# PEER gates by indirect writes into a DRAM table of experts, in place of a grid in SBUF

## The chip, the cores and the metric

One core of a Trainium2 chip. The metric is the device time of one execution of the program in microseconds (us); lower is better. Engines: TensorE (PE), VectorE (DVE), ScalarE (ACT), GpSimd (POOL) and SyncE (SP). SP, ACT and POOL issue DMAs.

## The reference

One decoder layer for 256 tokens of width 1024: two attention branches, a gated merge, then a PEER layer. This part is the PEER layer and what follows it:

```python
q = (ht @ w_pq).reshape(T, 8, 2, 128)
sub = einsum('thpc,hpnc->thpn', q, peer_keys)        # 128 keys per half
s_top, i_top = top_k(sub, 16)
cand_s = s_top[:, :, 0, :, None] + s_top[:, :, 1, None, :]   # 16 x 16 per head
cand_i = i_top[:, :, 0, :, None] * 128 + i_top[:, :, 1, None, :]
best_s, pos = top_k(cand_s, 16)
expert = take_along_axis(cand_i, pos)                # 8 heads x 16 = 128 slots per token
gate = softmax(best_s)
act = gelu(ht . peer_u[expert])
out = sum over slots of gate * act * peer_v[expert]
x = rms_norm(x + gt2 * out, g_final)
```

There are 16384 experts, numbered 128 i + j. A token picks 128 slots; two heads may pick the same expert, whose gates then add up.

## The kernel before, in words

The PEER layer is computed densely. The activations gelu(h . u) of all experts and all 256 tokens are made on PE, weighted by a gate that is zero where a token did not pick the expert, and multiplied by all of v. Experts go by blocks of 128 with one j and all i on the partitions: 128 blocks of u and 128 of v, each [128, 1024] float32 (512 KB), taken in 64 pairs. Every product is in three matmuls of high and low halves (`mm3`, L84 to L87), and each loaded block is split into those halves by one ACT copy (L81) and one DVE subtraction (L82).

1. **0 to 301 us**: adaLN, attention, merge, projection to queries.
2. **301 to 467 us, routing**, in two halves of 128 tokens (`tt`): scores (psub, L650), top 16 on DVE (`top16`, L631), ranks to indices (eq, sel). The result, per token and slot the indices i and j and the gate, is transposed (psel, L716) into `selT`. Between the pieces `u_some` (L589) issues pairs of u blocks: 2.5 units of routing work per pair (`PACE_R`).
3. **467 to 694 us, grid**: for 4 tokens at a time DVE builds one-hot matrices E, A (L746) and B (E times the gate in three bf16 pieces, L753); 12 matmuls pg (L737) per pair of tokens' blocks sum them into [i, token, j], and ACT copies that into the SBUF grid `G` (L740, 128 KB per partition). Two such steps stand between pairs of u blocks (`PACE_G` = 2).
4. **694 to 1081 us, v stage**: 64 pairs of v blocks in the order of a list `order`. `act_of` (L778) brings the activations of a pair, `weighted` (L786) multiplies them by the gates of G and splits the product, `v_mm` adds into four PSUM tiles `acc`. Within it 6 pairs of u blocks are still computed and used directly (j of 116 and above, `J0`); the 58 others were stored by ACT.
5. **to 1099 us**: the sum is scaled by gt2, added to x, normalized and stored. The row form of gt2 is made by 8 products `pgt` (L823) with diagonal matrices `dg` from DVE, within the last three pairs.

The lines that the steps touch:

```python
def u_spill(j):                                                              # L582
    a = upool.tile([P, 2, T], F32, tag="a", name=f"as{j}")
    nc.scalar.activation(a, upair(j, f"s{j}"), AF.Gelu_apprx_tanh)
    nc.scalar.dma_start(act_spill[j // 2], a.rearrange("p a t -> p (a t)"))
...
def act_of(j):                                                               # L778
    a = apl.tile([P, 2, T], F32, tag="a", name=f"a{j}")
    if j < J0:
        nc.sync.dma_start(a.rearrange("p a t -> p (a t)"), act_spill[j // 2])
    else:
        nc.scalar.activation(a, upair(j, f"m{j}"), AF.Gelu_apprx_tanh)
    return a
def weighted(j, a):                                                          # L786
    nc.vector.tensor_mul(a, a, G[:, :, j : j + 2].rearrange("p t s -> p s t"))
```

What sets the order: the program's order of instructions is made per engine by a scheduler, which may move an instruction ahead of others where its inputs allow. Each engine and each of the DMA-issuing queues then works strictly in order. SP loads u, v and the stored activations; a loaded block takes one of four buffers (`raw`), which is free again when the DVE subtraction has read it.

Of the kernel before, what the change touches and what calls it, by code (L numbers as in the profile page):

```python
# [18 lines left out]
P = 128  # L19
# [6 lines left out]
J0 = 116  # L26

PACE_R = 2.5
PACE_G = 2.0
# [5 lines left out]
def kernel(  # L35
# [32 lines left out]

    act_spill = dpool.tile([J0 // 2, P, 2 * T], F32, name="act_spill")
    x1_spill = dpool.tile([2, P, D], F32, name="x1_spill")  # L70
# [419 lines left out]
    for p in range(2):  # L490
        o = pm.tile([P, T], F32, tag="mm", name=f"pd{p}")
        for tt in range(2):
            rest = dilated(p, o, tt)
            gates(4 * p + 2 * tt)
            bg()
            rest()
            gates(4 * p + 2 * tt + 1)
            bg()
        put_o(o, 4 + p, f"d{p}")
# [81 lines left out]

    def u_spill(j):  # L582
        a = upool.tile([P, 2, T], F32, tag="a", name=f"as{j}")
        nc.scalar.activation(a, upair(j, f"s{j}"), AF.Gelu_apprx_tanh)
        nc.scalar.dma_start(act_spill[j // 2], a.rearrange("p a t -> p (a t)"))
# [3 lines left out]
    def u_some(share):  # L589
        spilled[1] += share  # L590
        while spilled[1] >= 1.0 and spilled[0] < J0:
            u_spill(spilled[0])
            spilled[0] += 2
            spilled[1] -= 1.0
# [12 lines left out]
    qT = rpool.tile([P, 16, T], F32, name="qT")  # L607
    ranks = rpool.tile([P, 16, P], BF16, name="ranks")
# [34 lines left out]
    for tt in range(2):  # L643
# [3 lines left out]
        for q in range(4):  # L647
# [11 lines left out]
            u_some(4.0 / PACE_R)  # L659
        nc.vector.tensor_copy(i_top, i_u)  # L660
# [53 lines left out]
        ps = pr_.tile([P, 3, P], F32, tag="t", name=f"psel{tt}")  # L714
        for x in range(3):
            nc.tensor.transpose(ps[:, x], sel[:, x].rearrange("p h k -> p (h k)"), ident)  # L716
        ts_ = slice(P * tt, P * tt + P)
        nc.scalar.activation(selT[:, 0:3, ts_], ps, AF.Copy)
        rest = rpool.tile([P, P], F32, tag="rk", bufs=2, name=f"rest{tt}")
        nc.vector.tensor_sub(rest, ps[:, 2], selT[:, 2, ts_])  # L720
        nc.vector.tensor_copy(selT[:, 3, ts_], rest)
        nc.vector.tensor_sub(selT[:, 4, ts_], rest, selT[:, 3, ts_])
    es_r.close()
    es_x.close()


    gpool = ctx.enter_context(tc.tile_pool(name="grid", bufs=1))
    G = gpool.tile([P, T, NJ], F32, name="G")
    es_g = ExitStack()
    opool = es_g.enter_context(tc.tile_pool(name="onehot", bufs=2))  # L730
    pg = es_g.enter_context(tc.tile_pool(name="pg", bufs=3, space=PSUM))
    def grid_mm(b, A, Bs):

        ps = pg.tile([P, 4, P], F32, tag="g", name=f"pg{b}")
        for t in range(4):
            for x in range(3):
                nc.tensor.matmul(  # L737
                    ps[:, t], A[:, :, t], Bs[t // 2][:, x, :, t % 2], start=(x == 0), stop=(x == 2)
                )
        nc.scalar.activation(G[:, 4 * b : 4 * b + 4], ps, AF.Copy)  # L740

    for b in range(T // 4):
        E = opool.tile([P, P, 4], BF16, tag="E", bufs=1, name=f"E{b}")
        A = opool.tile([P, P, 4], BF16, tag="A", bufs=2, name=f"A{b}")
        for x, M in ((1, E), (0, A)):
            nc.vector.tensor_tensor(  # L746
                M, selT[:, x, None, 4 * b : 4 * b + 4].to_broadcast([P, P, 4]), iota4, op=OP.is_equal
            )
        Bs = []
        for q in range(2):  # L750
            B = opool.tile([P, 3, P, 2], BF16, tag="B", bufs=4, name=f"B{b}_{q}")
            g = selT[:, 2:5, None, 4 * b + 2 * q : 4 * b + 2 * q + 2].to_broadcast([P, 3, P, 2])
            nc.vector.tensor_tensor(  # L753
                B, E[:, None, :, 2 * q : 2 * q + 2].to_broadcast([P, 3, P, 2]), g, op=OP.mult
            )
            Bs.append(B)
        grid_mm(b, A, Bs)
        u_some(1.0 / PACE_G)
    u_some(J0)
    es_g.close()  # L760
# [8 lines left out]
    direct, stored = list(range(J0, NJ, 2)), list(range(0, J0, 2))  # L769
    order = [direct.pop(0)]  # L770
    while direct or stored:
        if direct:
            order.append(direct.pop(0))
        for _ in range(-(-len(stored) // (len(direct) + 1))):
            order.append(stored.pop(0))
    n_pairs = len(order)

    def act_of(j):  # L778
        a = apl.tile([P, 2, T], F32, tag="a", name=f"a{j}")
        if j < J0:  # L780
            nc.sync.dma_start(a.rearrange("p a t -> p (a t)"), act_spill[j // 2])
        else:
            nc.scalar.activation(a, upair(j, f"m{j}"), AF.Gelu_apprx_tanh)
        return a

    def weighted(j, a):  # L786
        nc.vector.tensor_mul(a, a, G[:, :, j : j + 2].rearrange("p t s -> p s t"))  # L787
        wh = wpool.tile([P, 2, T], F32R, tag="wh", name=f"wh{j}")
        wl = wpool.tile([P, 2, T], F32R, tag="wl", name=f"wl{j}")
        split(wh, wl, a)  # L790
        return wh, wl
# [9 lines left out]
    for n, j in enumerate(order):  # L801
# [6 lines left out]
        if n == n_pairs - 3:  # L808
# [3 lines left out]
            ones = wpool.tile([P, P], F32, name="ones")  # L812
            nc.vector.memset(ones, 1.0)
            nc.sync.dma_start(gfb, g_final.to_broadcast([P, D]))
            nc.scalar.activation(gfb, gfb, AF.Copy, scale=float(D**0.5))
            nc.sync.dma_start(x1, x1_spill.rearrange("a p d -> p a d"))
            for q in range(2):
                ps = pp.tile([P, 4, P], F32, tag="pp", name=f"pgt{q}")
                for k in range(4):
                    dg = wpool.tile([P, P], F32, tag="dg", name=f"dg{q}{k}")  # L820
                    i = 40 + 4 * q + k
                    nc.vector.tensor_scalar(dg, ident, mod[:, i : i + 1], None, op0=OP.mult)
                    nc.tensor.matmul(ps[:, k], ones, dg, start=True, stop=True)  # L823
                nc.vector.tensor_copy(gtb[:, 512 * q : 512 * q + 512], ps.rearrange("p a b -> p (a b)"))
# [12 lines left out]
    st = wpool.tile([P, 2, 8], F32, tag="dg", name="st")  # L837
# [37 lines left out]
def _arrays(inputs):  # L875
# [48 lines left out]
    a["iota"] = np.tile(np.repeat(i, 4)[None, :], (P, 1)).astype(ml_dtypes.bfloat16)  # L924
# [29 lines left out]
```

## Time and profile before

| | |
|---|---|
| median of three runs | 1100.81 us (1100.40 to 1103.03) |
| the profiled execution | 1100.67 us, with a span of 1098.9 us |
| PE busy | 1063.5 us, 97% |
| DVE busy | 832.3 us, 76% |
| ACT busy | 557.4 us, 51% |
| POOL busy | 0.2 us |
| moved by DMA | 237.58 MB, mean 216 GB/s |

Busy shares are means over the stages above; what bounds a stage is read from that stage. Matmuls are pipelined, so the sum of their durations is more than the time they take; the distance between their starts is their pace.

### The profile page before, as it was taken

How to read it: one execution, taken by the hardware profiler on the slowest of the kernel's cores; microseconds unless marked ns; L12 is line 12 of the kernel's file. 1: busy time of each engine (PE TensorE's matmuls, PEld its weight loads, DVE VectorE, ACT ScalarE, POOL GpSimd, SP SyncE). 2: the span in 40 equal slices, each digit the busy share in tenths (PEclk: the TensorE clock that was granted, in tenths of full speed). 3: DMA queues.
4: the chain of work that ended last, by engine and by line, in shares of the span. 5: the costliest groups of instructions: out<-in, count | busy, mean ns of one | idle time of the engine just before them, and what ended most of it. 6: DMA issues, size and time to landing. Idle time of an engine off the chain costs nothing.

```text
span 1098.9 us, 19552 instructions
## 1 busy us (share of the span) xinstructions
PE 1063.5 (97%) x7672; PEld 973.4 (89%) x7674; DVE 832.3 (76%) x1539; ACT 557.4 (51%) x706; POOL 0.2 (0%) x4
## 2 busy tenths in 40 slices
PE   7889999998999999999999999999999999999986
PEld 4878988998999999999999999888888888878865
DVE  6777886776799799778777787676777677677675
ACT  5496344655465545545454454544444444445432
POOL 0000000000000000000000000000000000000000
PEclk9999999999999999999999999999999999999998
DMA  9965567365866766755555555567676666668751
GB/s 334 370 222 177 185 230 266 105 211 210 297 220 221 244 206 198 246 181 189 175 191 175 183 183 182 190 216 253 212 249 225 235 220 239 221 222 276 255 195 39
DMA packets 74206, 237.58 MB, mean 216 GB/s; under 512 B 8449, under 2 KB 8833, under 8 KB 73986
## 3 DMA queue, kind: packets, MB, share of 16 engines
q1 hardware_dynamic: 64898, 220.04, 59.1%
q10 hardware_dynamic: 9216, 16.29, 4.0%
q8 instruction: 60, 0.98, 0.4%
q14 instruction: 32, 0.26, 0.1%
HBM read 219.00 MB, written 17.30 MB: 215 GB/s over the span
## 4 chain that ended last, share of the span: by engine, by line
PE 69%; DMA 8%; DVE 5%; issue 3%; ACT 1%; DVEq 0%; SPq 0%; ACTq 0%
PE pus L85 10%; PE pus L86 10%; PE pus L87 10%; PE acc L87 7%; PE acc L86 7%; PE acc L85 7%; DMA a<-act_spill 6%; PE pg L737 4%; DVE l_v L82 1%; DVE wl L82 1%; DMA r_pq<-in_w_pq_dram 1%; PE p_g L85 1%; PE p_g L86 1%; PE pum L87 1%; PE pum L85 1%
## 5 line engine op out<-in xcount | busy, mean ns | idle before, releaser
L85 PE MATMUL pus<-hh_n,h_u 128*128 128x256 f32 x928 | 265.7, 286 | 0.0
L86 PE MATMUL pus<-hl_n,h_u 128*128 128x256 f32 x928 | 262.6, 283 | 0.0
L87 PE MATMUL pus<-hh_n,l_u 128*128 128x256 f32 x928 | 262.4, 283 | 0.0
L81 ACT ACTIVATE h_u<-r_u 128x1024 fp32r<-128x1024 f32 x128 | 135.8, 1061 | 179.4 <-PE pus L86 151.1
L87 PE MATMUL acc<-h_v,wl 128*128 128x512 f32 x512 | 200.9, 393 | 1.0 <-DVE wl L82 0.6
L86 PE MATMUL acc<-l_v,wh 128*128 128x512 f32 x512 | 200.8, 392 | 0.6 <-DVE l_v L82 0.6
L85 PE MATMUL acc<-h_v,wh 128*128 128x512 f32 x512 | 200.1, 391 | 0.0
L81 ACT ACTIVATE h_v<-r_v 128x1024 fp32r<-128x1024 f32 x128 | 134.9, 1055 | 113.7 <-PE acc L87 56.5
L86 PEld LDWEIGHTS pus<-hl_n,h_u 128*128 128x128 f32 x928 | 178.0, 192 | 0.0
L87 PEld LDWEIGHTS pus<-hh_n,l_u 128*128 128x128 f32 x928 | 177.9, 192 | 0.0
L82 DVE TENSOR_TENSOR l_u<-r_u,h_u 128x1024 fp32r<-128x1024 f32 x128 | 155.1, 1219 | 30.1 <-ACT h_u L81 29.9
L85 PEld LDWEIGHTS pus<-hh_n,h_u 128*128 128x128 f32 x928 | 177.8, 192 | 0.0
L82 DVE TENSOR_TENSOR l_v<-r_v,h_v 128x1024 fp32r<-128x1024 f32 x128 | 154.2, 1220 | 15.2 <-ACT h_v L81 15.2
L787 DVE TENSOR_TENSOR a<-a,G 128x512 f32<-128x512 f32 x64 | 70.3, 1099 | 98.1 <-DMA a<-act_spill 98.1
L87 PEld LDWEIGHTS acc<-h_v,wl 128*128 128x128 f32 x512 | 96.5, 189 | 23.7 <-DVE wl L82 4.1
L86 PEld LDWEIGHTS acc<-l_v,wh 128*128 128x128 f32 x512 | 96.7, 189 | 21.6 <-DVE l_v L82 1.9
L85 PEld LDWEIGHTS acc<-h_v,wh 128*128 128x128 f32 x512 | 96.6, 189 | 19.7
L753 DVE TENSOR_TENSOR B<-E,selT 128x768 bf16<-128x768 bf16 x128 | 68.1, 552 | 33.1 <-PE pg L737 33.1
L81 ACT ACTIVATE wh<-a 128x512 fp32r<-128x512 f32 x64 | 40.4, 631 | 81.1 <-PE acc L86 74.8
L151 DVE SCALAR_TENSOR_TENSOR junk<-ada,c_sb 128x1024 bf16<-128x1024 f32 x44 | 53.6, 1218 | 2.8 <-DMA ada<-in_w_ada_dram 2.7
L737 PE MATMUL pg<-B,A 128*128 128x128 bf16 x768 | 52.0, 222 | 1.0 <-DVE rest L720 1.0
L737 PEld LDWEIGHTS <-A 128*128 128x128 bf16 x768 | 46.9, 114 | 2.5 <-issue 1.0
(319 smaller groups left out, 1809.4 us busy)
## 6 DMA issues: line engine op xcount, KB each, us to landing
r_u<-in_u_dram SPq DMA_DIRECT2D x128, 512.0 KB, 3.6
r_v<-in_v_dram SPq DMA_DIRECT2D x128, 512.0 KB, 4.4
ada<-in_w_ada_dram SPq DMA_DIRECT2D x20, 1024.0 KB, 7.4
act_spill<-as ACTq DMA_DIRECT2D x58, 256.0 KB, 2.3
a<-act_spill SPq DMA_DIRECT2D x58, 256.0 KB, 3.7
r_g<-in_w_in_dram SPq DMA_DIRECT2D x16, 512.0 KB, 4.0
r_pq<-in_w_pq_dram SPq DMA_DIRECT2D x16, 512.0 KB, 6.3
r_first<-in_w_in_dram SPq DMA_DIRECT2D x8, 512.0 KB, 7.1
```

Of the source, the lines that this page charges most:

```text
L81: nc.scalar.activation(hi, src, AF.Copy)
L82: last_split[:] = [nc.vector.tensor_sub(lo, src, hi.bitcast(F32))]
L85: nc.tensor.matmul(ps, lh, rh, start=start, stop=False)
L86: nc.tensor.matmul(ps, lh, rl, start=False, stop=False)
L87: nc.tensor.matmul(ps, ll, rh, start=False, stop=stop)
L151: nc.vector.scalar_tensor_tensor(junk, raw[:, k], 1.0, c_sb, op0=OP.mult, op1=OP.mult, accum_out=mod[:, t + k : t + k + 1])
L737: nc.tensor.matmul(ps[:, t], A[:, :, t], Bs[t // 2][:, x, :, t % 2], start=(x == 0), stop=(x == 2))
L753: nc.vector.tensor_tensor(B, E[:, None, :, 2 * q : 2 * q + 2].to_broadcast([P, 3, P, 2]), g, op=OP.mult)
L787: nc.vector.tensor_mul(a, a, G[:, :, j : j + 2].rearrange("p t s -> p s t"))
```

## The change

The gates no longer make a grid. A DRAM table `ag` has a row of 512 float32 for every expert (2 KB), with four parts of 128: for each half of the tokens the activations (x = 0) and the gates (x = 1).

- 32 DMAs on POOL write zeros over all gate parts, 1024 pieces of 512 B each; 16 are issued in the attention, 16 with the first eight pairs of u blocks.
- ACT stores the activations of all 64 pairs into the table, two DMAs per pair, in pieces of 512 B. No pair is left for the v stage.
- Per half of the tokens DVE forms the expert's number of each slot, finds the first slot with the same number (`max_index`), and for each of the 128 slots sums the gates of the slots with the same number. Then POOL writes that slot's 128 sums, one per token, each to its own address of the table: 128 indirect DMAs of 128 single float32. A slot that repeats an earlier one writes to a spare place behind the table. `PACE_G` = 15 of these stand between pairs of u blocks.
- A load `a` brings activations and gates of a pair together (512 KB, 4 KB per partition; four buffers in place of two). It waits for all 256 indirect writes and its pair's own stores.
- The rows of gt2 are made in the routing (`gate_rows`), stored, and loaded at the end. The grid, its one-hot matrices and psel are gone.

```diff
-PACE_G = 2.0
+PACE_G = 15.0
...
+    ag = dpool.tile([NE + SPARE, ROW], F32, name="ag")
...
+    def clear(after):
+        j = blank.pop(0)
+        with tc.issue_after(after.ins):
+            for h in range(2):
+                o = nc.gpsimd.dma_start(
+                    ag_parts[:, j : j + 8, h, 1], zero[:, None, :].to_broadcast([P, 8, P])
+                )
...
     def u_spill(j):
-        nc.scalar.dma_start(act_spill[j // 2], a.rearrange("p a t -> p (a t)"))
+        for s in range(2):
+            o = nc.scalar.dma_start(ag_parts[:, j + s, :, 0], a[:, s].rearrange("p (h t) -> p h t", h=2))
...
+        if blank:
+            clear(made)
...
+    def gate_rows():
+        go = rpool.tile([P, D], F32, tag="xo", bufs=1, name="go")
+        for q in range(2):
+            ps = pr_.tile([P, 4, P], F32, tag="t", name=f"pgt{q}")
+            for k in range(4):
...
+                nc.vector.tensor_scalar(dg, ident, mod[:, i : i + 1], -1.0, op0=OP.mult, op1=OP.mult)
+                nc.tensor.matmul(ps[:, k], neg_one, dg, start=True, stop=True)
+            nc.scalar.activation(go[:, 512 * q : 512 * q + 512], ps.rearrange("p a b -> p (a b)"), AF.Copy)
+        nc.scalar.dma_start(x1_spill[2], go)
...
+        for k in range(0, P, 8):
+            nc.vector.max_index(seen[:, k : k + 8], num[:, k : k + 8], num)
...
+        for k in range(P):
+            same = rpool.tile([P, P], F32, tag="same", name=f"same{tt}_{k}")
+            nc.vector.scalar_tensor_tensor(
+                same, num, num[:, k : k + 1], gf, op0=OP.is_equal, op1=OP.mult, accum_out=tot[:, k : k + 1]
+            )
+            o = nc.gpsimd.indirect_dma_start(
+                out=ag_flat, out_offset=bass.IndirectOffsetOnAxis(ap=at_i[:, k : k + 1], axis=0),
+                in_=tot[:, k : k + 1], in_offset=None,
+            )
...
+            scatters.append(o.ins)
+            u_some(1.0 / PACE_G)
...
-        grid_mm(b, A, Bs)
-        u_some(1.0 / PACE_G)
-    u_some(J0)
+    u_some(NJ)
...
     def act_of(j):
-        a = apl.tile([P, 2, T], F32, tag="a", name=f"a{j}")
-        if j < J0:
-            nc.sync.dma_start(a.rearrange("p a t -> p (a t)"), act_spill[j // 2])
-        else:
-            nc.scalar.activation(a, upair(j, f"m{j}"), AF.Gelu_apprx_tanh)
+        a = apl.tile([P, 2, 2, 2, P], F32, tag="a", bufs=4, name=f"a{j}")
+        o = nc.sync.dma_start(a.rearrange("p s h x t -> p s (h x t)"), ag_pairs[:, j : j + 2])
+        for i in scatters + spills[j]:
+            tc.add_manual_dep(o.ins, i.name, data_dep)
         return a
```

The order of instructions changes in three places that the prediction speaks of.

POOL, the whole program, as it now is (`idle` is a tile of zeros, `tot` the sums, `at_i` the addresses; L212 is the clear, L788 the indirect write):

```order
L969 ISA
L969 MEMSET const-float32-0.0 128x1
L969 MEMSET const-float32-1.0 128x1
L969 MEMSET const-bfloat16-1.0 128x1
L969 MEMSET const-uint8-127 128x1
L975 UNCONDITIONAL_BRANCH
L212 DMA ag<-idle 128x8x128 x32
L788 DMA ag<-tot_4490,at_i_4488 8421376x1 x128
L788 DMA ag<-tot_6601,at_i_6599 8421376x1 x128
L975 UNCONDITIONAL_BRANCH
L975 ISA
```

Before, POOL had the first six and the last of these and no DMA. Each DMA from the ninth on also waits for the eighth before it to land.

SP around the first load of activations, before:

```order
L91 DMA r_u118_8990<-in_u_dram 128x1024
L91 DMA r_u119_9020<-in_u_dram 128x1024
L91 DMA r_v116_9063<-in_v_dram 128x1024
L91 DMA r_v117_9069<-in_v_dram 128x1024
L91 DMA r_v118_9106<-in_v_dram 128x1024
L91 DMA r_v119_9112<-in_v_dram 128x1024
L91 DMA r_v0_9149<-in_v_dram 128x1024
L91 DMA r_v1_9155<-in_v_dram 128x1024
L91 DMA r_v2_9192<-in_v_dram 128x1024
L781 DMA a0_9061<-act_spill_69 128x512
```

and now (r_u96 is block 96 of u; a0, a2 the activations and gates of the first pairs):

```order
L97 DMA r_u96_7771<-in_u_dram 128x1024
L97 DMA r_u97_7801<-in_u_dram 128x1024
L97 DMA r_u98_7836<-in_u_dram 128x1024
L97 DMA r_u99_7866<-in_u_dram 128x1024
L813 DMA a0_8824<-ag_69 128x1024
L97 DMA r_u100_7901<-in_u_dram 128x1024
L813 DMA a2_8826<-ag_69 128x1024
L97 DMA r_u101_7931<-in_u_dram 128x1024
L813 DMA a4_8840<-ag_69 128x1024
L97 DMA r_u102_7966<-in_u_dram 128x1024
L813 DMA a6_8884<-ag_69 128x1024
L97 DMA r_u103_7996<-in_u_dram 128x1024
```

The first load of activations stood behind all loads of u but those of the direct pairs; it now stands ahead of r_u100 to r_u127, and eight such loads are spread among these.

DVE while the second half's slots are summed (L785 the sums, l_u the low half of a u block), where the grid's E, A and B stood between the l_u:

```order
L785 SCALAR_TENSOR_TENSOR same1_50_6947,tot1_6601<-num1_6574,sel1_6267 128x128
L88 TENSOR_TENSOR l_u79_7003<-r_u79_7000,h_u79_7002 128x1024
L785 SCALAR_TENSOR_TENSOR same1_51_6950,tot1_6601<-num1_6574,sel1_6267 128x128
L785 SCALAR_TENSOR_TENSOR same1_52_6953,tot1_6601<-num1_6574,sel1_6267 128x128
L785 SCALAR_TENSOR_TENSOR same1_53_6956,tot1_6601<-num1_6574,sel1_6267 128x128
L785 SCALAR_TENSOR_TENSOR same1_54_6959,tot1_6601<-num1_6574,sel1_6267 128x128
L785 SCALAR_TENSOR_TENSOR same1_55_6962,tot1_6601<-num1_6574,sel1_6267 128x128
L88 TENSOR_TENSOR l_u80_7083<-r_u80_7080,h_u80_7082 128x1024
```

Five sums stand between two subtractions, from block 70 to block 95; the first half's stand so from block 26 to block 48.

## Rows read from the trace of the kernel before

**Rows 1.** The page: busy time by engine; the span in 40 slices.

```profile
PE 1063.5 (97%) x7672; PEld 973.4 (89%) x7674; DVE 832.3 (76%) x1539; ACT 557.4 (51%) x706; POOL 0.2 (0%) x4
...
PE   7889999998999999999999999999999999999986
...
GB/s 334 370 222 177 185 230 266 105 211 210 297 220 221 244 206 198 246 181 189 175 191 175 183 183 182 190 216 253 212 249 225 235 220 239 221 222 276 255 195 39
```

**Rows 2.** Busy time by stage: from:to, length, then each engine; clock, DMA share.

```profile
301.00:467.00 166.00, 165.83 (x1388) 165.73 (x1387) 147.25 (x513) 93.42 (x106) 0.00 (x0) 1.00 0.67 222
467.00:694.00 227.00, 226.20 (x2252) 224.77 (x2252) 178.98 (x312) 113.52 (x159) 0.00 (x0) 1.00 0.55 183
694.00:1081.00 387.00, 380.61 (x1792) 317.35 (x1790) 267.51 (x275) 182.01 (x207) 0.00 (x0) 0.99 0.67 224
```

**Rows 3.** The chain that ended last, in order of time: start, length, what.

```profile
467.80 0.88 PE pg L737 x12
...
472.19 1.46 PE pg L737 x24
...
479.45 1.47 PE pg L737 x24
...
690.07 2.36 PE pg L737 x36
```

**Rows 4.** Groups by line, whole span: count, busy us, mean ns, idle before.

```profile
L753 DVE TENSOR_TENSOR B<-E,selT 128x768 bf16<-128x768 bf16 x128 | 68.1, 552 | 33.1 <-PE pg L737 33.1
...
L740 ACT ACTIVATE G<-pg 128x512 f32<-128x512 f32 x64 | 35.4, 594 | 1.5 <-PE pg L737 1.3 <-ACT G L740 0.2
...
L746 DVE TENSOR_TENSOR E<-selT,iota 128x512 bf16<-128x512 bf16 x64 | 27.0, 421 | 1.1
```

**Rows 5.** Groups by line: DVE in the routing, and ACT's split of u.

```profile
L82 DVE TENSOR_TENSOR l_u<-r_u,h_u 128x1024 fp32r<-128x1024 f32 x57 | 68.4, 1217 | 17.2 <-ACT h_u L81 16.9
...
L641 DVE FIND_INDEX8 i_u<-s_top,sub 128x8 uint32<-128x128 f32 x32 | 8.5, 284 | 0.0
...
L694 DVE SCALAR_TENSOR_TENSOR rk<-pn,pw 128x128 f32<-128x128 uint32 x4 | 1.1, 283 | 0.0
...
L81 ACT ACTIVATE h_u<-r_u 128x1024 fp32r<-128x1024 f32 x128 | 135.8, 1061 | 179.4 <-PE pus L86 151.1
```

**Rows 6.** PE in order of time near the end, and a table as rows 2.

```profile
1062.37 0.39 PE L85 MATMUL acc<-h_v,wh 128*128 128x512 f32 x1
1062.60 0.39 PE L86 MATMUL acc<-l_v,wh 128*128 128x512 f32 x1
...
1068.77 0.80 PE L823 MATMUL pgt<-dg,ones 128*128 128x128 f32 x2 [4.87 <-DVE dg L822]
...
1068.80:1074.30 5.50, 5.50 (x16) 4.63 (x17) 3.22 (x7) 0.00 (x0) 0.00 (x0) 0.50 0.01 2
```

**Rows 7.** Waits, longest in total: who for whom, us, times, longest.

```profile
DVE a L787 <- DMA a<-act_spill: 98.1, 57, 3.6
```

**Rows 8.** Instructions of pus and psel with first and last start; psub's group.

```profile
L85 PE MATMUL pus<-hh_n,h_u x928: 279/283/365, 301.9 to 689.6; 128*128 128x256 f32 x186
...
L716 PE MATMUL psel<-ident,sel x6: 272/272/273, 379.6 to 464.3; 128*128 128x128 f32 x6
...
L650 PE MATMUL psub<-kT,qT 128*128 128x128 f32 x64 | 8.4, 275 | 0.0
```

**Rows 9.** DMA queues, issues to landing, and the issuing queues' own time (ns).

```profile
q10 hardware_dynamic: 9216, 16.29, 4.0%
...
r_u<-in_u_dram SPq DMA_DIRECT2D x128, 512.0 KB, 3.6
...
act_spill<-as ACTq DMA_DIRECT2D x58, 256.0 KB, 2.3
...
L585 ACTq DMA_DIRECT2D act_spill<-as x58: 326/326/334, 310.9 to 691.6; - x58
...
940.18 1.46 SPq L91 DMA_DIRECT2D r_v<-in_v_dram  x2
```

More of the change, by code (lines that the diff above doesn't have):

```diff
@@ L196, in bg @@
                     background.pop(0)()
+    zero = idle.bitcast(F32)[:, 0:P]
+    blank = list(range(0, NJ, 8))
+    def clear(after):
[5 more added lines that the diff above has]
+                )
+                tc.declare_no_dep(o.ins, group="clear", reason="other places")
+                tc.add_to_no_dep_group("clear", o.ins)
     def rms(sq, name):
@@ L580, in upair @@
         return ps
+    spills, scatters = {}, []
     def u_spill(j):
[L583 to L585 removed]
+        a = upool.tile([P, 2, T], F32, tag="a", bufs=2, name=f"as{j}")
+        made = nc.scalar.activation(a, upair(j, f"s{j}"), AF.Gelu_apprx_tanh)
+        spills[j] = []
+        for s in range(2):
+            o = nc.scalar.dma_start(ag_parts[:, j + s, :, 0], a[:, s].rearrange("p (h t) -> p h t", h=2))
+            for g in ("clear", "acts", "gates"):
+                tc.declare_no_dep(o.ins, group=g, reason="other places")
+            tc.add_to_no_dep_group("acts", o.ins)
+            spills[j].append(o.ins)
+        if blank:
+            clear(made)
     spilled = [0, 0.0]
@@ L590, in u_some @@
         spilled[1] += share
-        while spilled[1] >= 1.0 and spilled[0] < J0:
+        while spilled[1] >= 1.0 and spilled[0] < NJ:
             u_spill(spilled[0])
@@ L713 @@
         nc.vector.tensor_tensor(ge, ge, gsum[:, :, None].to_broadcast([P, 8, 16]), op=OP.mult)
[L714 to L720, printed above, removed]
@@ new lines @@
+        nc.vector.tensor_sub(at_f, at_f, spare)
+        nc.vector.tensor_mul(at_f, at_f, fst)
+        at_i = sel_pool.tile([P, P], I32, tag="at_i", bufs=2, name=f"at_i{tt}")
+        nc.vector.tensor_add(at_i, at_f, spare)
+        tot = sel_pool.tile([P, P], F32, tag="tot", bufs=2, name=f"tot{tt}")
+        gf = ge.rearrange("p h k -> p (h k)")
+        for k in range(P):
+            same = rpool.tile([P, P], F32, tag="same", name=f"same{tt}_{k}")
+            nc.vector.scalar_tensor_tensor(
+                same, num, num[:, k : k + 1], gf, op0=OP.is_equal, op1=OP.mult, accum_out=tot[:, k : k + 1]
+            )
+            o = nc.gpsimd.indirect_dma_start(
+                out=ag_flat, out_offset=bass.IndirectOffsetOnAxis(ap=at_i[:, k : k + 1], axis=0),
+                in_=tot[:, k : k + 1], in_offset=None,
+            )
+            for g in ("acts", "gates"):
+                tc.declare_no_dep(o.ins, group=g, reason="other places")
+            tc.add_to_no_dep_group("gates", o.ins)
+            scatters.append(o.ins)
+            u_some(1.0 / PACE_G)
@@ L723 @@
     es_r.close()
     es_x.close()
[L727 to L740, printed above, removed]
@@ L811 @@
             x1 = hpool.tile([P, 2, D], F32, tag="hl", name="x1")
-            ones = wpool.tile([P, P], F32, name="ones")
-            nc.vector.memset(ones, 1.0)
             nc.sync.dma_start(gfb, g_final.to_broadcast([P, D]))
             nc.scalar.activation(gfb, gfb, AF.Copy, scale=float(D**0.5))
[L816 to L824, printed above, removed]
+            nc.sync.dma_start(gtb, x1_spill[2])
+            nc.sync.dma_start(x1, x1_spill[0:2].rearrange("a p d -> p a d"))
         todo = [(w, vs)] if n < n_pairs - 1 else todo + [(w, vs)]
@@ L923, in _arrays @@
     a["cst"] = np.concatenate([np.eye(P), -tri, np.tile(i[None, 0:16], (P, 1))], axis=1).astype(np.float32)
-    a["iota"] = np.tile(np.repeat(i, 4)[None, :], (P, 1)).astype(ml_dtypes.bfloat16)
+    at = [P + 2 * P * h + i for h in range(2)] + [NE * ROW + P * (P * h + i) for h in range(2)]
+    a["iota"] = np.concatenate([np.tile(i[None, :], (P, 1)), np.stack(at, axis=1)], axis=1).astype(np.float32)
     inv = np.float32(10000.0) ** (-np.arange(32, dtype=np.float32) / np.float32(32))
```

66 lines of the change are left out of this document (32 added, 34 removed).

## The prediction

> **What bounds the kernel now.** I read the page's first two parts, then a table by stage, then the chain in order of time, and last the operations that the change replaces. TensorE (PE) is busy 97% of the span and at 9 tenths in nearly every slice [rows 1]. By stage it is the same everywhere the change works, at the full granted clock (1.00, 2.4 GHz) [rows 2]: 165.83 of 166 us while the routing runs, 226.20 of 227 us while the gate grid is built, 380.61 of 387 us while v is multiplied. So an operation on PE between 301 and 1081 us costs its own time, and work on VectorE (DVE) or ScalarE (ACT) costs nothing until it holds PE up. DVE is the nearest: 147 of 166 us in the routing. The DMA engines are 0.55 to 0.67 busy there.
>
> The chain from 467 us on shows it in detail [rows 3]: 24 matmuls of the grid (pg) every 7.26 us for 1.46 us, and between them one pair of u blocks. So a pair of u blocks takes 7.26 - 1.46 = 5.8 us of PE, one block 2.9 us. Two blocks are 1 MB of u.
>
> **The grid's removal.** 768 matmuls pg leave PE. The first and last of their pieces in the chain are 0.88 us (12) and 2.36 us (36), with 30 of 24 between them at 1.46 us: 0.88 + 2.36 + 43.8 = 47 us, all of it on the bound. DVE loses E, A and B (27.0 us, as much again, and 68.1) and ACT the copies to G (35.4 us) [rows 4]; both had slack, so that is worth nothing by itself. It makes room for what is new.
>
> **What DVE gets.** Per half of the tokens: 16 searches of 0.284 us, six 128-wide operations and 128 scalar_tensor_tensor at 0.283 us (the nearest row) [rows 5]: 4.5 + 1.7 + 36.2 = 42 us, 84 us in all against 122 us removed. The order puts five of the 128 between two subtractions l_u: 5 x 0.283 + 1.22 = 2.63 us, under the 2.9 us of a u block. So 128 take 128/5 x 2.9 = 74 us at PE's pace and PE isn't held. If the cover is thinner than that, each DVE overrun costs PE directly; I allow 0 to 20 us in the range and nothing in the sum.
>
> **The tail.** Eight pgt products wait for DVE within the last v pairs: PE stands 4.87 us, and after it the granted clock is 0.50, the 1.2 GHz level, for 5.5 us [rows 6]. Half of 5.5 is lost, 2.7 us. Moved into the routing, the same products have other matmuls around them. That is -7.6 us; their own PE time only moves.
>
> **The v stage.** Six pairs of u blocks move ahead of it and cost PE the same there. The load a doubles to 512 KB. DVE waited 98.1 us for a [rows 7], but PE was covered, so four buffers in place of two give nothing. 1.57 MB per pair in 24 x 0.2265 = 5.44 us (acc matmuls start 0.23 us apart in [rows 6]) is 289 GB/s; the opening slices moved 334 and 370 GB/s [rows 1], so it fits, without much room.
>
> **The new wait.** All 64 loads a now need all 256 indirect writes, and these are a serial queue on POOL, which issued no DMA before (0.2 us busy). SP is in order too: the first a stands ahead of r_u100, with 28 loads of u behind it. Until the last indirect write has landed, no u block from 100 on is loaded and PE runs dry. The deadline: the first u block starts at 301.9 us [rows 8]; 100 blocks x 2.9 us, 8.4 us of psub matmuls [rows 8] and about 1 us of pgt end at 601 us; block 100 needs 3.6 us to land, 1.06 on ACT and 1.22 on DVE before that [rows 5, 9]. So SP must be free by about **595 us**.
>
> When can the writes run? Routing of the first half ends at 379.6 us (psel) [rows 8]; with 7 us of new DVE work, 387 us. The second half ended at 464.3 us; 128/15 = 8.5 u pairs (49.5 us) and some 9 us more come before it: 523 us. With c us of POOL per indirect write, the last lands 2.3 us [rows 9] after the later of 523 + 128c and 387 + 256c.
>
> What is c? No row shows it. From below: a DMA of 128 rows that ACT issues takes 0.326 us of its queue [rows 9]; from above, one write at a time, 2.3 us from issue to landing. POOL builds addresses by program and reads an index per row, so it should cost more than either hardware issue; the nearest row is SP's 0.73 us for 128 rows of 4 KB (two in 1.46 us) [rows 9]. I take **0.85 us**: 523 + 109 + 2.3 = 634 us, a stall of 39 us. At 0.326 the DVE pace (0.57) rules and there is none; at 2.3 us it ends at 978 us, a stall of 383.
>
> The Trainium skill (DMA: Bandwidth & Descriptors, Specifications) gives about 1 us to the first byte from POOL against 0.6 from SP or ACT; by that the sum would be some 1104 us, no longer faster. No run here shows it.
>
> The 32 clears also go to POOL: 1024 rows of 512 B each. By the ACT issue (0.326 us for 128) one is 2.6 us, 83 us in all; half are issued from about 150 us on, half with the first eight u pairs, up to 350 us. They fit ahead of 387 us up to 7 us apiece; past that every write slips. ACT issues two stores of 256 rows per pair, some 1.3 us, in place of one of 0.33 and two G copies of 0.59: covered by its idle half [rows 2].
>
> **Sum**, against the profiled execution's 1100.67 us (the median of the runs is 1100.81): -47 grid, -7.6 tail, +39 stall = **1085 us**.
>
> **Rivals.** (1) *POOL keeps up*: c at or under 0.55, all hidden: 1046 us. For it: eight writes may be in flight, and 0.326 us is possible for hardware. Against: POOL is software.
>
> (2) *SP held past break-even* (slower): the same wait with a higher price. The stall eats the 54.6 us gained when 523 + 128c + 2.3 - 595 = 54.6, c = 0.97. At 1.2 us POOL is behind from the first half on: 387 + 307 + 2 - 595 = 101 us, 1147 us; at 1.44, 1210 us. For it: 28 u loads sit behind one wait, and nothing in the u stage after it can replace them.
>
> (3) *DVE holds POOL off.* DVE will be about 95% busy beside the writes. If a write has to wait for the operation that runs (0.28 or 1.22 us, 0.6 on average), c is 1.45 and the time 387 + 371 + 2.3 - 595 = 165 us over 1046: 1211 us. The rows speak for it only in that DVE has so little idle time.
> The rule is the Trainium skill's (SBUF — State Buffer, SBUF: two separate sides): POOL can't write descriptors while DVE runs a two-port operation. It names copies in a fast mode; l_u at 1.22 us for 1024 isn't one, so I give it little.
>
> (4) *DMA engines become the bound.* One u pair with its store used 0.55 x 7.26 = 4.0 us of them [rows 2, 3]. ACT's queue took 4.0% of 16 engines for 9216 packets, mostly of 2 KB [rows 9]: 0.04 x 16 x 1098.9 / 9216 = 76 ns each. 512 B cost 19 ns by bytes, 76 by count; at 38 a pair needs 3.4 (4.0 less its own store of 128) + 512 x 0.038/16 = 4.6 us and an indirect write 128 x 0.038/16 = 0.3 us. From 387 to 595 us that is 36 x 4.6 + 256 x 0.3 = 242 us in 208: 34 us late, 1080 us, in the same stretch as the stall and not on top of it. At 76 ns the excess is some 158 us.
>
> **How the numbers follow.** The measurement tells 0.3%, 3.3 us, from no change. Forecast (c from 0.55 to 0.94) 0.28; rival 4 at its middle 0.08; rival 1 0.14: faster 0.50. A stall within 3.3 us of the gain 0.05. Rival 2 0.33 and rival 3 0.12: slower 0.45. Both signs have weight, so: the forecast's own range is 1048 to 1097 us; the 8-in-10 range is 1045 us (everything hidden) to 1210 us (c = 1.44), and leaves out the dearest prices on POOL.
>
> **What would show it.** POOL's DMAs back to back from about 387 us, 128 of them per half; PE with a gap of some 40 us near 600 us while the chain reads POOL, then a; no pg; 24 acc matmuls per 5.4 us in the v stage; no gap at pgt. A gap before 500 us, many short waits for r_u, or a DMA share near 1 would speak for rival 4; no gap for rival 1. DVE operations grown longer beside POOL would speak for rival 3. I am wrong if the time lies outside the range or the gap has another cause than the wait for the indirect writes.

## The result and the profile after

The changed kernel takes **1230.65 us** (median of 4 runs, 1229.45 to 1231.26) against 1101.92 of the kernel before on the same chip: 1.116 times as long, 95% interval 1.113 to 1.119. The profiled execution has a span of 1227.7 us, 128.8 more than before. In two later sets of runs, on two chips, the same program took 1314.8 and 1322.6 us (e2 and c1 below): it has two courses. The one that the prediction was put against, the calm one, is read first; the other is called the slow course below.

The page, as [rows 1]: busy time, and the span in 40 slices.

```profile
PE 1021.1 (83%) x6898; PEld 934.1 (76%) x6900; DVE 802.6 (65%) x1864; ACT 526.1 (43%) x642; POOL 316.2 (26%) x292
...
PE   5679999998999997999960000599999999999996
...
POOL 4310000000000577888777777100000000000000
...
GB/s 351 402 401 308 138 214 250 154 194 207 293 207 228 222 222 141 231 226 221 221 119 0 1 0 0 273 278 225 291 321 288 289 291 289 291 286 294 286 247 69
```

PE lacks 42 us of its former busy time, and now stands empty for four slices while POOL works on. Three marks of PE's line, the first pus, the first acc and the end, tell where the time went. The instructions of these groups with first and last start, before:

```profile
L85 PE MATMUL acc<-h_v,wh x512: 387/389/628, 703.8 to 1088.8; 128*128 128x512 f32 x171
```

and after, with pgt, the writes, the clears and the sums:

```profile
L91 PE MATMUL pus<-hh_n,h_u x1024: 278/283/583, 332.8 to 869.3; 128*128 128x256 f32 x171
...
L91 PE MATMUL acc<-h_v,wh x512: 389/389/398, 869.6 to 1217.5; 128*128 128x512 f32 x171
...
L647 PE MATMUL pgt<-dg,neg_one x16: 273/275/377, 370.1 to 376.0; 128*128 128x128 f32 x16
...
L788 POOL DMA_INDIRECT ag<-tot,at_i x256: 957/962/5252, 408.7 to 772.9; - x128
...
L212 POOL DMA_DIRECT2D ag<-idle x32: 887/887/1079, 1.5 to 72.0; - x32
...
L785 DVE SCALAR_TENSOR_TENSOR same<-num,sel x256: 325/352/397, 407.3 to 623.4; 128x128 f32<-128x128 f32 x128
```

- To the first pus: 332.8 against 301.9 [rows 8], **+30.9**. The clears run from 1.5 us on, among the first weight loads, and GB/s stands at 402 and 401 there.
- From there to the first acc: 536.8 against 401.9, **+134.9**.
- From there to the end: 358.1 against 395.1, **-37.0**: the tail's 7.6 us, and the direct u pairs (29 us) that now lie ahead.

The table by stage, as [rows 2]:

```profile
390.00:480.00 90.00, 90.00 (x754) 90.00 (x753) 86.93 (x347) 43.34 (x51) 56.63 (x49) 1.00 0.78 220
480.00:530.00 50.00, 43.13 (x339) 42.81 (x338) 49.90 (x216) 22.73 (x25) 41.47 (x29) 0.90 0.62 188
530.00:580.00 50.00, 50.00 (x419) 50.00 (x418) 48.36 (x182) 25.15 (x29) 40.24 (x33) 1.00 0.80 224
...
640.00:700.00 60.00, 0.00 (x0) 0.00 (x0) 0.00 (x0) 0.00 (x0) 45.62 (x48) 0.50 0.02 0
...
840.00:1210.00 370.00, 369.96 (x1750) 311.13 (x1749) 244.74 (x258) 179.47 (x204) 0.00 (x0) 1.00 0.82 278
```

from the waits, who waited for whom, us, times, longest:

```profile
SPq L813 <- DMA ag<-tot,at_i: 149.7, 4, 146.0
```

and from the page, PE's products of u: busy, mean ns, idle time before them and what ended it:

```profile
L91 PE MATMUL pus<-hh_n,h_u 128*128 128x256 f32 x1024 | 292.4, 286 | 146.5 <-ACT as L608 146.5
...
L93 PE MATMUL pus<-hh_n,l_u 128*128 128x256 f32 x1024 | 291.7, 285 | 6.9 <-DVE l_u L88 6.9
```

Beside the u blocks POOL gets 33 writes into 50 us, 1.5 us each; with everything else empty 48 into 60, 1.27 us. SP stands 146 us before the first load of a, the u loads behind it wait, and PE is empty for 146.5 us. A second, smaller gap of 6.9 us lies between 480 and 530 us, where DVE is full (49.90 of 50) and PE waits for l_u. The v stage is full (369.96 of 370). Why a write takes 1.5 us beside the u blocks shows in order of time, start and length:

```profile
429.25 0.96 POOL L788 DMA_INDIRECT ag<-tot,at_i  x1 [0.31 <-DVE same L785]
...
429.89 1.22 DVE L88 TENSOR_TENSOR l_u<-r_u,h_u 128x1024 fp32r<-128x1024 f32 x1
...
430.52 1.43 POOL L788 DMA_INDIRECT ag<-tot,at_i  x1 [0.30 <-issue]
...
432.25 0.96 POOL L788 DMA_INDIRECT ag<-tot,at_i  x1 [0.30 <-DVE same L785]
```

A write is 0.96 us, and 0.30 us pass before the next; one that begins beside l_u is 1.43 us. The subtraction here ends at 431.11 and the held write at 431.95, 0.84 us later. So it is through the trace: nearly all of some 60 writes that begin beside l_u end 0.83 to 0.84 us behind a subtraction, however long that takes (the longest write, 5.25 us, was held through more than one), while writes that begin beside a sum take 0.96 us. Two writes fall to each u block.

### The profile page after: what moved, and what is told of

It is laid out like the page before. It is cut to its first block, busy times and chain, and to the rows that moved or that the text cites. A ratio compares the mean times of both kernels' runs of the same rounds, so it can differ in the third digit from the quotient of the medians.

```text
span 1227.7 us, 18780 instructions
## 1 busy us (share of the span) xinstructions
PE 1021.1 (83%) x6898; PEld 934.1 (76%) x6900; DVE 802.6 (65%) x1864; ACT 526.1 (43%) x642; POOL 316.2 (26%) x292
## 4 chain that ended last, share of the span: by engine, by line
PE 57%; DVE 12%; POOL 8%; issue 5%; DMA 1%; ACT 1%; POOLq 0%; ACTq 0%; DVEq 0%; SPq 0%
PE acc L92 9%; PE acc L93 9%; PE acc L91 9%; POOL ag L788 8%; PE pus L93 6%; PE pus L91 6%; PE pus L92 6%; DVE same L785 4%; DVE l_u L88 4%; PE p_pq L91 1%; PE p_pq L92 1%; PE p_pq L93 1%; PE p_g L91 1%; PE p_g L92 1%; DMA ag<-tot,at_i 1%
## 5 line engine op out<-in xcount | busy, mean ns | idle before, releaser
L91 PE MATMUL pus<-hh_n,h_u 128*128 128x256 f32 x1024 | 292.4, 286 | 146.5 <-ACT as L608 146.5
L788 POOL DMA_INDIRECT ag<-tot,at_i x256 | 287.4, 1123 | 413.6 <-PE pus L92 335.9
L91 PEld LDWEIGHTS pus<-hh_n,h_u 128*128 128x128 f32 x1024 | 198.4, 194 | 146.9 <-ACT as L608 146.8
L93 PE MATMUL pus<-hh_n,l_u 128*128 128x256 f32 x1024 | 291.7, 285 | 6.9 <-DVE l_u L88 6.9
L92 PE MATMUL pus<-hl_n,h_u 128*128 128x256 f32 x1024 | 291.4, 285 | 0.0
L92 PEld LDWEIGHTS pus<-hl_n,h_u 128*128 128x128 f32 x1024 | 198.4, 194 | 0.0
L820 DVE TENSOR_TENSOR w<-a 128x512 f32<-128x512 f32 x64 | 44.3, 692 | 155.2 <-DMA a<-ag 153.1
L87 ACT ACTIVATE wh<-w 128x512 fp32r<-128x512 f32 x64 | 40.4, 632 | 240.0 <-DVE w L820 150.7
L785 DVE SCALAR_TENSOR_TENSOR same<-num,sel 128x128 f32<-128x128 f32 x256 | 90.1, 352 | 6.6
L88 DVE TENSOR_TENSOR wl<-w,wh 128x512 fp32r<-128x512 f32 x64 | 44.3, 692 | 55.3 <-ACT wh L87 55.2
```

The lines of the kernel that those rows point to most:

```text
L87: nc.scalar.activation(hi, src, AF.Copy)
L88: last_split[:] = [nc.vector.tensor_sub(lo, src, hi.bitcast(F32))]
L91: nc.tensor.matmul(ps, lh, rh, start=start, stop=False)
L92: nc.tensor.matmul(ps, lh, rl, start=False, stop=False)
L93: nc.tensor.matmul(ps, ll, rh, start=False, stop=stop)
L785: nc.vector.scalar_tensor_tensor(same, num, num[:, k : k + 1], gf, op0=OP.is_equal, op1=OP.mult, accum_out=tot[:, k : k + 1])
```

## The experiments

**e1, the last gate's rows alone.** The kernel before with `gate_rows()`, its call in the routing, and `gtb` loaded from `x1_spill[2]` in place of the products in the tail.

> The kernel before with one part of the change alone: the last gate's rows (pgt) laid out in the routing, stored with the rows of x and loaded at the end; grid and stores as before. My theory: the tail's 7.6 us go, and the eight matmuls cost the routing under 2 us: 1094 (1092 to 1097). Rival: the tail waits for the loads of the rows as it waited for pgt, and the time stays at 1100 to 1103.

Measured: 1096.2 us against 1100.9, ratio 0.995 (0.993 to 0.997), inside the range. The products now stand in the routing, where PE waits 1.9 us for dg in place of 4.87 at the end,

```profile
PE pgt L617 <- DVE dg L616: 1.9, 1, 1.9
```

and the gain is about 5 of the 7.6 us. This part alone is a version that beats both kernels, by 0.5% against the kernel before.

**e2 and c1, the same program twice.**

```diff
-        o = nc.sync.dma_start(a.rearrange("p s h x t -> p s (h x t)"), ag_pairs[:, j : j + 2])
+        with tc.issue_after(last_u[0].ins):
+            o = nc.sync.dma_start(a.rearrange("p s h x t -> p s (h x t)"), ag_pairs[:, j : j + 2])
```

> The changed kernel, the loads of a ordered behind the last u block. My theory (SP stood before the first a load, and with it the 28 u loads behind it): PE works through the last u blocks while POOL writes; last write landed at 775 to 790 (later if l_u, which now runs on DVE to the end, lengthens the writes beside it as in 430 to 446), first acc 7 us behind it, then 358 us: 1143 to 1158. Rival (the u blocks waited for something else, say for ACT's stores, and SP's order is no cause): the idle time of PE stays and the time is 1220 to 1235.

Here last_u is the activation of the last u pair. The lines moved no load: queue by queue the program is the changed kernel's, so e2 tests nothing of SP's place. It took 1314.8 us (1309.3 to 1315.9, ratio 1.193, 1.189 to 1.196). So the changed kernel was run again as it is:

> The changed kernel itself once more, because e2's program came out the same as its, queue by queue (the order of issue that the edit asks for moved no load), and yet took 1314.8 in place of 1230.7. Theory A (one program, two courses: once the writes follow each other freely, without being held by an l_u or by a sum, all other engines come down to an instruction in 1.4 us; which course is taken hangs on how the first writes fall): near 1230 or near 1315, nothing between. Theory B (the extra time belongs to something in e2): 1228 to 1233.

1322.6 us (1315.4 to 1326.0), ratio 1.200 (1.194 to 1.205): theory A's numbers, and nothing of e2's own is the cause. The table by stage of c1:

```profile
410.00:450.00 40.00, 24.48 (x136) 20.85 (x136) 16.02 (x59) 7.71 (x9) 26.31 (x27) 0.70 0.34 87
...
570.00:610.00 40.00, 12.02 (x50) 10.43 (x51) 5.39 (x37) 3.35 (x5) 20.66 (x22) 0.52 0.04 7
```

and c1 in order of time, PE and POOL:

```profile
584.72 0.96 POOL L788 DMA_INDIRECT ag<-tot,at_i  x1 [0.30 <-issue]
585.98 0.96 POOL L788 DMA_INDIRECT ag<-tot,at_i  x1 [0.31 <-issue]
...
588.00 0.37 PE L92 MATMUL pus<-hl_n,h_u 128*128 128x256 f32 x1 [2.43 <-issue]
590.80 0.37 PE L93 MATMUL pus<-hh_n,l_u 128*128 128x256 f32 x1 [2.43 <-issue]
```

and DVE in e2:

```profile
539.31 0.09 DVE L685 MATCH_VALUE_LOAD i_u<-s_top,sub 128x8 f32 x1 [1.10 <-DVE s_top L683]
539.39 0.28 DVE L685 FIND_INDEX8 i_u<-s_top,sub 128x8 uint32<-128x128 f32 x1
540.71 0.09 DVE L685 MATCH_VALUE_LOAD i_u<-s_top,sub 128x8 f32 x1 [1.04 <-DVE i_u L685]
```

and PE's idle time on c1's page:

```profile
L91 PE MATMUL pus<-hh_n,h_u 128*128 128x256 f32 x1024 | 304.9, 298 | 62.6 <-issue 61.9
L93 PE MATMUL pus<-hh_n,l_u 128*128 128x256 f32 x1024 | 305.9, 299 | 55.7 <-issue 54.0
L92 PE MATMUL pus<-hl_n,h_u 128*128 128x256 f32 x1024 | 303.6, 296 | 52.9 <-issue 52.0
```

In these stretches POOL writes every 1.27 us, held by nobody. PE does a matmul in 2.80 us, each with its weight load, and DVE a search in 1.40 us. PE waits for nothing that the profile shows ("issue"), 168 us in all; DVE's rows name only its own instruction before. The DMA engines are 0.04 busy. With PE so slow few l_u come to hold POOL, so, as I read it, the course keeps itself up. In the calm course PE did 754 matmuls in 90 us and had no such idle time in its u work. The long wait of SP before the first load of a is gone from c1: with PE slow, u work lasts beyond the last write.

**e4, the clears later.** Each zero tile is now written by DVE in the dilated attention, where its four clears wait for it.

```diff
+        zt = xpool.tile([P, P], F32, tag="zero", bufs=2, name=f"zero{len(blank)}")
+        with tc.issue_after(after.ins):
+            nc.vector.memset(zt, 0.0)
+        zero = zt
+        clear(after)
+        clear(after)
...
-            clear(anchor[0])
+            clear2(anchor[0])
```

> The changed kernel, its 32 clears held back to the dilated attention by zero tiles that DVE writes there (two tiles, written anew for every four clears), order of SP as in the changed kernel. My theory (the opening lost its 31 us to the clears, which ran beside the first weight loads): first pus back at 302 to 306, the writes start 27 to 31 us earlier, and so does all behind them: 1198 to 1206. Rival (the clears cost as much wherever they run, because the DMA engines have the same work to do): 1225 to 1235 with first pus near 330. Rival (the opening is slow for another reason): the same time, with PE idle at 20 to 75 us as in the changed kernel.

1293.0 us (ratio 1.175, 1.172 to 1.178): the slow course, 22 us below e2 on the same chip. The forecasts of its time assumed the calm course, so the start of the u work has to answer. The stretch 25 to 50 us, first of the changed kernel,

```profile
25.00:50.00 25.00, 17.20 (x101) 13.78 (x99) 11.34 (x19) 8.16 (x14) 7.99 (x9) 0.80 1.02 402
```

then of e4, its clears, and its products of u:

```profile
25.00:50.00 25.00, 21.38 (x159) 20.36 (x159) 20.42 (x46) 9.56 (x16) 0.00 (x0) 0.93 0.92 347
...
L212 POOL DMA_DIRECT2D ag<-zero x32: 885/885/1077, 143.0 to 214.9; - x32
...
L91 PE MATMUL pus<-hh_n,h_u x1024: 275/283/581, 316.6 to 923.7; 128*128 128x256 f32 x171
```

The opening is whole again, so the clears were its loss; but the first pus is at 316.6, not 302 to 306: in the attention the clears cost 14.7 us, about half of what they cost in the opening.

**e6, without the sums; e7, half of the writes.**

```diff
+        nc.vector.tensor_copy(tot, gf)
...
-            nc.vector.scalar_tensor_tensor(
-                same, num, num[:, k : k + 1], gf, op0=OP.is_equal, op1=OP.mult, accum_out=tot[:, k : k + 1]
-            )
```

> The changed kernel without the 256 sums over equal experts: each slot writes its own gate, so a token's twice-chosen expert gets one gate in place of the sum; writes, clears and SP's order stay. It takes 256 x 0.43 us off DVE at 407 to 623 us. Theory A (POOL's own price of 0.96 + 0.30 us, lengthened by 0.47 us when a write begins beside an l_u): two writes for each u block of 2.7 us while u runs, then 1.27 us each: last write at 745 to 755 in place of 773, time 1203 to 1215. Theory B (the sums are what lengthens the writes): 1.27 us from the start, last write at 730 to 738, time 1187 to 1198. Theory C (the price is POOL's alone, DVE without effect): 1.43 us as before, 1225 to 1232.

The four runs lie far apart: 1336.6 us, and 1366.8 to 1377.8. Even the fastest is 22 us above e2's median, so none of the three theories came. Theory B's idea, that the sums lengthen the writes, is answered by the trace of the changed kernel above: beside a sum a write takes its 0.96 us. What the sums do is make POOL wait for them. Without that wait POOL runs freely more often; in the profile, which is of one of the three longer runs, PE's idle time by "issue" before its u products is 251 us, against c1's 168.

```diff
+            if k % 2:
+                continue
             o = nc.gpsimd.indirect_dma_start(
```

> The changed kernel with every second write left out (the gates of the odd slots are never stored; sums, clears and order stay). Simple price theory (SP waits for the last write, at 1.43 us each): the last write is landed near 640, PE waits about 15 us instead of 146: 1090 to 1105. Theory A (freely running writes hold all engines): with sums twice as many as writes, POOL waits for the sums more often and runs freely less: between 1095 and 1180, with stretches of slow PE only where POOL's pitch is 1.27.

1138.5 us, ratio 1.035 (1.032 to 1.038): above the range of the simple price theory, inside theory A's. PE doesn't wait for the last write any more (its u work ends at 777 us, the last write starts at 677.7), but stands 29 us by "issue" before its u products. Its first slow stretch, 418 to 427 us, lies where four writes in a row come 1.26 us apart, and ends with a 4.1 us wait of POOL for a sum. This is 184 us below c1 on the same chip, but only 92 below the calm course, so no price of one write follows from it.

**e10, a real wait behind u; e11 and e12, a pause before each write; e13, with late clears too.**

```diff
-        for i in scatters + spills[j]:
+        for i in [last_u[0].ins] + scatters + spills[j]:
...
+            rest = sel_pool.tile([P, 256], F32, tag="rest", bufs=4, name=f"rest{tt}_{k}")
+            nc.gpsimd.tensor_copy(rest, tot[:, k : k + 1].to_broadcast([P, 256]))
...
-                in_=tot[:, k : k + 1], in_offset=None,
+                in_=rest[:, 0:1], in_offset=None,
```

> The changed kernel with a real wait: each load of a also waits for the last l_u, so SP has all u loads and three of v ahead of the first a. Simple theory (SP's place alone): last write 775 to 790, first acc 7 us behind, 358 us to the end: 1143 to 1158. Theory A: in the calm course the same; in the other course the writes end near 850 and the 28 u loads are hidden: 1215 to 1245. A rival to both: 1230 or 1315 unchanged, since PE has no u work left when the writes end late.

> As e10, and POOL copies the gate out to 256 columns before each write and writes from there, so that two writes are never nearer than the copy allows (my estimate 0.3 to 0.6 us more for each write). Theory A: the other engines keep their pace beside the writes, PE's u blocks end at 715 to 735 without slow stretches, and the writes end at 811 to 888: 1175 to 1255, the same in each run. Theory C (each write holds the others by itself, dense or not): PE is as slow beside them as in e2, with waits of 1.4 us an instruction.

> As e11 with a copy of 32 columns instead of 256. e11's copies took 0.41 us alone and made the pitch 1.67 us where DVE was idle. Theory A: whatever keeps the pitch over some 1.45 us keeps the engines at their pace; the last write at 781 to 830, the end 366 us behind it: 1147 to 1196. If the pause is too short, the slow course is back: 1300 to 1325.

> As e11 with a copy of 96 columns, and the clears held back to the dilated attention as in e4. First pus at 316 and the first write at 392 (both as in e4, 16 us before the changed kernel's); pitch 1.55 to 1.75 us: last write at 789 to 840, the end 366 us behind it: 1155 to 1206. If the engines are held: over 1260.

In e10 last_u is the last l_u, so the loads of a now wait for it. e10: 1318.2 us (ratio 1.195, 1.191 to 1.198), c1's time: its rival holds. In the slow course PE has u work to the end, and SP's place is no matter. What SP's place alone is worth in the calm course no run shows. e11: 1280.5 us (1.164, 1.160 to 1.167), e12: 1240.0 (1.126, 1.124 to 1.128), e13: 1233.0 (1.120, 1.118 to 1.123), all three above their ranges, but without PE's idle time by "issue" in the u work: it is at its pace beside the writes, but for short waits for l_u. The table by stage of e12, and its writes and acc:

```profile
530.00:570.00 40.00, 40.00 (x336) 40.00 (x335) 38.93 (x139) 21.13 (x24) 34.44 (x41) 1.00 0.76 223
...
750.00:800.00 50.00, 0.00 (x0) 0.00 (x0) 0.00 (x0) 0.00 (x0) 40.56 (x68) 0.50 0.02 1
```

```profile
L791 POOL DMA_INDIRECT ag<-rest,at_i x256: 982/985/5272, 411.2 to 872.1; - x128
...
L91 PE MATMUL acc<-h_v,wh x512: 387/389/793, 879.3 to 1230.1; 128*128 128x512 f32 x171
```

Copies and writes together are 68 in 50 us with DVE empty, a pitch of 1.47, as expected; beside DVE 41 in 40 us, 1.95, which I hadn't expected: l_u holds the copies as well as the writes. The first acc comes 7.2 us behind the last write, in e11 7.1 (912.0 to 919.1). So with the u work out of the way the last write sets the end, and a pause buys PE's pace with POOL's time. None of the three is below the calm course's 1230.65 us.

**e5, e15 to e19: the writes by themselves.** e15 puts 64 writes beside the v stage of the kernel before, waited for by nobody; e16 spreads their places; e17 pauses before each. e18 leaves out 15 pairs of v and does the matmuls of the 21st pair 16 times, so PE has a stretch without loads or DVE beside e16's writes, with as much work in all; e19 has e17's pauses there. In the cut the first lines are those of e15, the last those of e18.

```diff
+        if n == 20:
+            nc.vector.tensor_copy(one, w[0][:, 0, 0:1].bitcast(F32))
+            for i in range(64):
+                o = nc.gpsimd.indirect_dma_start(
+                    out=spot, out_offset=bass.IndirectOffsetOnAxis(ap=at_i[:, i : i + 1], axis=0), in_=one, in_offset=None
+                )
...
+    order = order[:21] + order[37:42] + [order[27]] + order[42:]
...
-            for s in range(2):
...
+            for i in range(16 if n == 20 else 1):
+                for s in range(2):
```

> The kernel before, and in its v stage 64 indirect writes of one column to a spare table, one behind the other, from the 21st pair on; nobody waits for them (64 small operations of DVE that make their places come early and may cost up to 4 us). Theory A (dense writes hold the other engines by themselves): PE comes down to an instruction in 1.4 us while they run, which is at least 64 x 1.27 = 81 us: 1150 to 1185. Theory C (the writes cost time only through the waits behind them): 1100 to 1106. Between the two (each l_v holds POOL off, as l_u does in the calm course, and PE goes on): 1104 to 1125.

> The changed kernel with each indirect write in place of its kind by a plain DMA of POOL: the same column of 128 gates, to 128 neighbouring places of the spare rows, so no gate reaches its expert (that part is left out). Waits, clears and order stay. Theory A1 (any dense row of POOL's DMAs of one element a partition holds the engines): 1230 to 1325, with matmuls at 1.4 us and more between. Theory A2 (the indirect form does it): no slow stretch; if a write costs 0.9 to 1.0 us in all, the writes end before the first load of a and the time is 1100.8 + 31 - 47 - 8 = 1077 (1070 to 1100).

e15: 1166.5 us, ratio 1.060 (1.057 to 1.064), in A's range for another reason. Its DMA issues from 850 to 920 us, KB each and us to landing:

```profile
r_v<-in_v_dram SPq DMA_DIRECT2D x11, 512.0 KB, 13.8
```

In the kernel before the same loads land in 4.5 us there. With neighbouring places the loads are what suffers. e5, whose places are neighbours too, has it as well: 1264.6 us (1.147, 1.143 to 1.151), DMA share 0.91 and 1.01 in the two stretches of 40 us from 410 us on, and loads of u that land after 14.6 us there. So e5 can't tell A1 from A2, and e15 can't tell A from C.

> e15 with its 64 writes at places over 2 KB apart instead of neighbouring ones. Theory A (dense writes hold the other engines' instructions): while they run (64 x 1.27 = 81 us at least) PE, ACT and DVE come down to an instruction in 1.4 us with the DMA engines nearly idle: 1150 to 1185. Theory C (they cost time only through waits): loads land as in the kernel before, 1100 to 1108. Between (l_v and the sums of w hold POOL off often enough): 1108 to 1130.

> e16 with POOL copying 32 columns before each write, as in e12. Theory A with density as its cause: no slow stretch, 1100 to 1112. If each write holds the others by itself: as e16.

1103.3 and 1103.1 us, each 1.001 (1.000 to 1.003): nothing lost. In e16 l_v and the other operations on two tensors hold POOL again and again, 64 writes in 100 us, never more than four at 1.27 us in a row. So the unbroken row was still untested.

> e16 with 15 pairs of the v stage left out and the 24 x 2 matmuls of the 21st pair done 16 times in their place: for some 85 us PE needs no load and no operation of DVE or ACT, DVE is idle, and the 64 writes run beside it without a hold at 1.27 us. PE's work in all is that of the kernel before. Theory A (writes that follow each other freely hold the other engines' instructions): PE falls to a matmul in 2.8 us (with its weight load, 1.4 us each) while they run: 1150 to 1185. Theory D (the slow course comes from the waits between POOL, DVE and PE, not from the writes alone): no gap in PE: 1090 to 1108.

> e18 with POOL copying 32 columns before each write. Theory A with density as the cause: PE keeps its pace: 1090 to 1108. Theory D: the same as e18, 1090 to 1108. If each write holds PE by itself: as e18 above 1140.

e18: 1157.3 us, ratio 1.050 (1.047 to 1.053); e19: 1099.2, ratio 0.998 (0.996 to 0.999). The table of e18,

```profile
836.00:846.00 10.00, 10.00 (x46) 8.29 (x45) 0.00 (x0) 0.00 (x0) 7.56 (x9) 1.00 0.02 0
846.00:850.00 4.00, 3.41 (x14) 2.28 (x13) 0.00 (x0) 0.00 (x0) 3.08 (x4) 1.00 0.02 0
850.00:854.00 4.00, 1.28 (x3) 0.34 (x3) 0.00 (x0) 0.00 (x0) 3.08 (x4) 0.95 0.02 0
...
862.00:880.00 18.00, 3.67 (x7) 2.02 (x7) 0.00 (x0) 0.00 (x0) 13.73 (x15) 0.50 0.02 2
```

the same in order of time,

```profile
865.84 0.58 PE L91 MATMUL acc<-h_v,wl 128*128 128x512 f32 x1 [2.20 <-issue]
868.64 0.58 PE L89 MATMUL acc<-h_v,wh 128*128 128x512 f32 x1 [2.21 <-issue]
```

and the table of e19:

```profile
860.00:880.00 20.00, 20.00 (x90) 16.54 (x90) 0.00 (x0) 0.00 (x0) 16.39 (x28) 1.00 0.02 1
```

This settles it: PE needs no load and no other engine here, and writes that follow each other without a hold still bring it down to a matmul in 2.80 us; with a pause it keeps its pace. After the last hold of a write (828.8 us) PE went on at full pace for some 20 us, then fell; the granted clock, 1.00 up to there, was 0.50 (1.2 GHz) only behind that, so it is not the cause. Whether the pause helps by the longer pitch or by the other kind of operation, these runs don't tell.

## Why the prediction was wrong

- *The grid and the tail*: right. pg is gone, the products pgt stand at 370 us between other matmuls, and e1 shows the tail's part, about 5 of 7.6 us.
- *The new wait*: right in its place, and mis-sized. SP stood before the first load of a from 629 us on (146 us up to its issue at 775.2); 595 and the opening's 31 make 626. The second stretch's +134.9, with the grid's 47 put back and the 29 us of the direct pairs taken off, is 153 us: 146.5 of this wait and 6.9 of the gap by DVE below. So the stall was **146 us, not 39**. The term that failed is c: "I take 0.85 us"; it was 1.27 us alone, and over all 256 writes (408.7 to 773.9) **1.43 us**. With 1.43 the prediction's own formula gives 387 + 366 + 2.3 - 595 = 160; the writes began at 408.7 us, 9 us earlier than 387 and the opening's 31, and that is most of the rest. So rival 2 came, at the end of its range: 1046 + 160 = 1206, and the opening on top 1237, against 1230.65.
- *Why c was too low*: the nearest row, SP's 0.73 us [rows 9], was misread. Its 1.46 us hold two issues and the wait between them; by itself an issue takes 0.33 us in the kernel before, like ACT's 0.326:

```profile
L91 SPq DMA_DIRECT2D r_v<-in_v_dram x128: 327/328/904, 682.2 to 1064.7; - x128
```

  So no row of the kernel before priced a write of POOL near 0.85 us. SP's queue is also another one (hardware_dynamic in the profile, POOL's q0 software_dynamic). And a write has 0.30 us between it and the next besides its own 0.96.
- *Rival 3*, where l_u "isn't one, so I give it little": it is one. A write that begins beside it takes 0.47 us more, and beside u the writes come 1.5 us apart, not 1.27. So rival 3's price (1.45) came true as well; it and rival 2 were one case. The prediction went by the copies in a fast mode alone. The Trainium skill (SBUF — State Buffer, SBUF: two separate sides) also names DVE operations with two SBUF inputs, which shut out a GpSimd operation that reads SBUF. The trace agrees for l_u, which reads two (1.43 us in place of 0.96), and not for the sums, which read two as well and leave a write at 0.96 us.
- *The clears*: "half are issued from about 150 us on" failed. The order of issue set no time: nothing made them wait, so POOL sent all 32 from 1.5 us on. "They fit" became +30.9 us.
- *DVE's cost at nothing*: nearly right beside the writes of each half, where PE was full (390 to 480 and 530 to 580 us), though a sum is 0.35 us and 0.08 to read it out instead of 0.283. Between them, where the second half's searches and the sums meet, DVE was full and PE waited 6.9 us; the allowance of 0 to 20 us held that.
- *Rival 4* didn't come: DMA share 0.78 to 0.80 beside the writes.
- The range ended at 1210 because it took the clears at nothing; with their 31 us it would have held the time. It had no case at all for the slow course.

## What to carry to other kernels

A serial queue of small operations that is new to an engine has no row to be priced by: take the whole range as the forecast, and look for the loads that stand behind its last wait. An order of issue is no wait; work that must not run early needs something to wait for. Where POOL writes in a dense row, leave pauses or don't do it beside work that has to keep its pace. And measure a changed program in more than one set of runs: the first set of four didn't show the second course.

## What the runs showed that I hadn't expected

- Indirect writes of POOL every 1.27 us slow the issue of PE and DVE to one instruction in 1.40 us, whatever its size: matmuls of 128, 256 and 512 columns (2.80 us with their weight load) and DVE's searches alike. A hold by l_u every 3 us (the calm course) or a copy before each write (e19) kept them free. Why this is so, no run tells; that PE goes on for some 20 us first (e18) looks as if it lived on a store of instructions, but that is a guess, and in e7 it fell some 9 us after the first write.
- One program had two courses, 1229 to 1231 and 1309 to 1326 us, and kept to one within a set of runs (4 each of the kernel, e2 and c1). The slow one came on two chips; what settles the course, and whether the chip has a part in it, is open.
- 64 writes of 128 neighbouring elements (e15) made loads beside them land after 13.8 us and not 4.5; the same writes over 2 KB apart cost nothing (e16). The Trainium skill (DMA: Bandwidth & Descriptors, Specifications) says that for transfers below 512 B a DMA engine does a read-modify-write. All of these are 4 B, so the runs add that it is the neighbours that hurt; whether the read-modify-write is the reason, no run shows.
